# The first half's normalized input kept in DRAM across the turn of a hybrid SSD and S5 block

## The chip, the cores and the metric

One core of a Trainium2 chip runs the whole kernel. Its engines are TensorE (PE, with its weight loads shown as PEld), VectorE (DVE), ScalarE (ACT), GpSimd (POOL) and SyncE (SP, which here only issues DMAs). Each works through its own queue in order, and waits on semaphores for the others. The metric is the device time of one execution, in microseconds (us); lower is better.

## The reference

One encoder block on 2048 tokens of width 1024, all in float32:

```
h  = RMSNorm(x) * norm_w
p  = h @ W_in                    # columns: SSD z | SSD x,B,C | dt fwd,bwd | S5 u
y1 = SSD heads: conv(x,B,C), chunked scan per direction over 16 chunks of 128 tokens,
     D skip, SiLU(z) gate, RMSNorm
y2 = S5 groups: 16 channels, 64 complex states, scan per direction, GELU, GLU, RMSNorm
x  = x + concat(y1, y2) @ W_out
x  = x + ConvGLU-FFN(RMSNorm(x))
out = RMSNorm(x)
```

The change touches only how h reaches the product with W_in a second time.

## The kernel before

A product in float32 precision is made of three products of two-part numbers: each operand is split into a high part (`hh`, `wh`) and a low part (`hl`, `wl`), and lines L444 to L446 multiply high with high, low with high and high with low. The tiles `ht = (hh, hl)` hold both parts of h, transposed (128 partitions, 8 blocks of features, 1026 tokens), that is, one half of the sequence at a time. There is room for one pair only.

**Stage one.** `norm_block` (L479) takes 512 tokens: it loads four tiles of x, normalizes them, transposes them on PE (L500) and writes the high part from ACT (L503) and the low part from DVE (L504). It runs for blocks 0 and 1, then for blocks 2 and 3, which overwrite the tiles; after each block `u_dt` computes the S5 input and the SSD step sizes. At its end `ht` holds tokens 1024 to 2047, half 1.

**Half 1.** `group` (L804) runs for four groups. Each has four `conv_tile` (projection, convolution, SiLU; L672), then eight `ssd_unit` (L741), one for each chunk, from the last chunk backwards. `z_tile` (L698) projects the gate. A unit loads `rw` (two tiles of 256 KB, L747) and `eb` (L751) on SP's queue, adds a mask to `rw` (L753, on DVE in half 1), takes the exponential on ACT (L764), and then PE, DVE and ACT pass its pieces on: transposes `ptb` (L756, L757), `pyd` (L770, L776), `pst` (L791), stores `y_d` (L783) and `sf_d` (L796), again on SP's queue. `rw` and `eb` have two buffers.

**The S5 recurrence.** Beside half 1, POOL runs `recur`: 126 steps of four operations each (L347 to L350) on the array `s5V`. Then `store_states` writes `s5V` to DRAM with 16 DMAs of 256 KB that POOL issues (L356).

**The turn.** `norm_again` (L506, called for two blocks at the end of half 1) makes h of tokens 0 to 1023 again: x is loaded (L519) into tiles borrowed from others (`xa`, `zt`, `wraw`, `rb`), scaled by the kept factors (L522, L524), transposed (L529) and split (L532 on ACT, L533 on DVE). `xa` has a pool of its own, `s5xa`, which is opened within the same scope as `s5V`.

**Half 0.** The pool `s5o` is opened when the scope of `s5V` and `xa` has ended, and takes the same space. `out_setup` loads `s5gw` into it (L364, eight DMAs on SP's queue), and `outputs`, called eight times through half 0, loads `s5tz`, `s5st`, `s5uTo` and `s5ot` (L375 to L384, SP's queue) and multiplies them on PE (`s5py`, L386; `s5pgl`, L400). Groups and gate tiles run as in half 1, now on tokens 0 to 1023. Then come the output product and the FFN, which are not touched.

**What sets the order.** The code above is not the order on the engines. A scheduler places every instruction by a simulated timeline and by priorities (`tc.high_priority`), when the data and, in that timeline, the space of its tile are free; what it finds is each engine's fixed queue. On the chip an engine then waits at the head of its queue, whatever stands behind.

Of the kernel before, what the change touches and what calls it, by code (L numbers as in the profile page):

```python
# [9 lines left out]
F32 = mybir.dt.float32  # L10
F32R = mybir.dt.float32r
I32 = mybir.dt.int32
AF = mybir.ActivationFunctionType
ALU = mybir.AluOpType
# [3 lines left out]
P = 128  # L18
L = 2048
D = 1024  # L20
# [396 lines left out]
class Block:  # L417
# [40 lines left out]
    def dram(self, dr):  # L458
        t = lambda name, shape, dt=F32: dr.tile(shape, dt, name=name)
        self.ud = t("u_d", [NG5, 2, P, P])  # L460
        self.ys_d = t("ys_d", [S5W, 2, 8, P])
        self.acs_d = t("acs_d", [16, 32, P])
        self.eac_d = t("eac_d", [16, 32, P])
        self.dec_d = t("dec_d", [16, 32])
        self.ct_d = t("ct_d", [4, P, L])
        self.y_d = t("y_d", [16, P, 8, P])
        self.z_d = t("z_d", [8, P, L])
        self.sf_d = t("sf_d", [16, P, 4, 256])
        self.x2_d = t("x2_d", [L, D])
        self.hop_d = [t(f"hop{i}_d", [P, 8, 4, 512]) for i in range(2)]  # L470
        self.act_d = t("act_d", [P, self.NF, L])
        self.wt_d = t("wt_d", [P, 11, 4, 512])
        self.yp_d = [t(f"yp{i}_d", [L, D]) for i in range(2)]


    def new_ht(self, pool):
# [26 lines left out]
            nc.scalar.activation(hi, pt, AF.Copy, scale=w)  # L503
            nc.vector.scalar_tensor_tensor(lo, pt, w, hi.bitcast(F32), ALU.mult, ALU.subtract)  # L504

    def norm_again(self, xp, wp, ps, ht, tb, off):  # L506
        nc = self.nc
        xt = []
        for i in range(4):
            if i == 0:  # L510
                t = xp.tile([P, D], F32, name="xa")
            elif i == 1:
                t = wp.tile([P, D], F32, name="zt", bufs=1)
            elif tb == 0:
                t = wp.tile([P, D], F32, name="wraw", bufs=2)
            else:
                t = self.rbp.tile([P, 1028], F32, name="rb", bufs=2)[:, 0:D]
            r0 = 512 * tb + 128 * i
            nc.sync.dma_start(t, self.A["x"][0, r0:r0 + 128, :])  # L519
            r = self.rs0[:, 4 * tb + i:4 * tb + i + 1]  # L520
            if i % 2:
                nc.vector.tensor_scalar(t, t, r, None, ALU.mult)  # L522
            else:
                nc.scalar.activation(t, t, AF.Copy, scale=r)  # L524
            xt.append(t)
        for k in range(8):
            pt = ps.tile([P, 512], F32, name="pt0", tag="mm")
            for i in range(4):
                nc.tensor.transpose(pt[:, 128 * i:128 * i + 128], xt[i][:, 128 * k:128 * k + 128], self.ident)  # L529
            w = self.nmw[:, k:k + 1]  # L530
            hi, lo = ht[0][:, k, off:off + 512], ht[1][:, k, off:off + 512]
            nc.scalar.activation(hi, pt, AF.Copy, scale=w)  # L532
            nc.vector.scalar_tensor_tensor(lo, pt, w, hi.bitcast(F32), ALU.mult, ALU.subtract)  # L533

    def u_weights(self, sp, wp):
        nc = self.nc
# [671 lines left out]
def hybrid_block_kernel(ctx: ExitStack, tc: tile.TileContext, *aps):  # L1208
    nc = tc.nc
    A = dict(zip(_INS, aps[:-1]))  # L1210
    b = Block(nc, tc, A, aps[-1])
    pool = tc.tile_pool
# [5 lines left out]
    with ExitStack() as mix:  # L1218
# [6 lines left out]
        ps, p5 = (psg.enter_context(pool(name=n, bufs=2, space=PSUM)) for n in ("psmm", "ps5"))  # L1225
# [3 lines left out]
        wp = lw.enter_context(pool(name="wp", bufs=1))  # L1229
# [3 lines left out]
        ht = b.new_ht(hp)  # L1233
# [3 lines left out]
        with pool(name="s0", bufs=1) as sp, right("s5cs") as cs:  # L1237
            with right("s5prm") as sr:
                b.norm_block(sp, wp, pp, ht, 0, 2)
                b.u_weights(sp, wp)  # L1240
                p0 = tc.cur_priority
                soon = lambda: tc.high_priority(offset=tc.cur_priority - p0)
                b.u_dt(sp, ps, ht, 0, 2)
                with soon():
                    b.norm_block(sp, wp, pp, ht, 1, 514)
                b.u_dt(sp, ps, ht, 1, 514)
                with soon():
                    for i in range(2):
                        nc.scalar.copy(ht[i][:, :, 0:2], ht[i][:, :, 1024:1026].bitcast(F32))
                for j in (2, 3):  # L1250
                    with soon():
                        b.norm_block(sp, wp, pp, ht, j, 512 * j - 1022)
                    b.u_dt(sp, ps, ht, j, 512 * j - 1022)
                with soon():
                    s5.params(cs, sr)
                    b.main_consts(mk, sr, s5.pst)
            with right("s5tab") as wk:
                with soon():
                    for k in range(NK5):
                        s5.tables(wk, k)  # L1260
                for m in range(ZA):
                    b.z_tile(wp, ps, ht, 1, m)
        late = rs.enter_context(right("late"))
        mp = rs.enter_context(right("mp"))
        with pool(name="s5v", bufs=1) as vp, ExitStack() as xs:
            off = tc.cur_priority - p0
            with tc.high_priority(offset=off), pool(name="dts", bufs=1) as sp:
                b.dt_stage(late, sp, ps)
                with pool(name="s5vw", bufs=1) as wk:
                    s5.toeplitz(*[wk.tile([P, 1024], F32, name="s5xi", bufs=3)[0:16, 0:512].rearrange(  # L1270
                        "p (g o) -> p g o", o=16) for _ in range(2)])
                    s5.inputs(vp, wk)
            sp = rs.enter_context(right("sp"))
            xp = xs.enter_context(pool(name="s5xa", bufs=1))
            b.masks(late)
            b.sb = late.tile([P, 4, 256], F32, name="sb")
            p0 = tc.cur_priority
            for g in range(GA):
                if g == GA - 1:
                    p3 = tc.cur_priority  # L1280
                b.group(mp, wp, sp, ps, pp, ht, 1, g)
                for m in ZB[g]:
                    b.z_tile(wp, ps, ht, 1, m)
            p1 = tc.cur_priority
            s5.recur(vp, lambda j: tc.high_priority(offset=tc.cur_priority - p0 - int(RS * (p1 - p0) * j / P)))
            s5.store_states()
            with tc.high_priority(offset=tc.cur_priority - p3):
                for j in range(2):
                    b.norm_again(xp, wp, ps, ht, j, 2 + 512 * j)
        with right("s5o") as so:  # L1290
            s5.out_setup(so)
            for g in range(4):
# [20 lines left out]
        ps = psb.enter_context(pool(name="psb", bufs=4, space=PSUM))  # L1313
# [70 lines left out]
```

## Time and profile before

| | us |
|---|---|
| median of 3 runs (2914.89 to 2917.51) | 2915.84 |
| the profiled execution | 2897.39 |
| its span in the trace | 2895.6 |
| PE busy in it | 2691.0 (93%) |
| DVE busy | 2192.7 (76%) |
| ACT busy | 1362.3 (47%) |
| POOL busy | 656.6 (23%) |

The trace is of the profiled execution, whose span is 1.8 us shorter than its time. Busy shares are means over stages with different limits; what counts for this change is the stretch of some 150 us around the turn, read engine by engine. In the views a row of a timeline is: start, duration, engine, line, operation, output tile and input tiles, and how many were joined into the row; brackets at its end give how long the engine had been idle before it, and for whom it waited.

### The profile page before, as it was taken

What the parts mean: (1) busy time and instruction counts of PE and PEld (TensorE: products, weight loads), DVE (VectorE), ACT (ScalarE), POOL (GpSimd) and SP (SyncE); (2) the same over time, 40 slices, a digit from 0 to 9 for tenths busy, and PEclk for the clock granted to TensorE, in tenths of its full rate; (3) what the DMA queues carried; (4) which work ended last, traced back from release to release, by engine and by line L of the source; (5) the groups of instructions that cost most, each with busy time, mean ns of one, the idle gap of its engine ahead of it and who ended that gap; (6) DMA issues with size and microseconds to landing.
All of it is one profiled execution on the core that took longest, in us unless ns stands there. A gap on an engine that the chain in (4) does not pass through costs nothing. (4 is left out here: it accounts for less than half of the span.)

```text
span 2895.6 us, 37272 instructions
## 1 busy us (share of the span) xinstructions
PE 2691.0 (93%) x12952; PEld 2177.5 (75%) x12952; DVE 2192.7 (76%) x3247; ACT 1362.3 (47%) x2325; POOL 656.6 (23%) x1133
## 2 busy tenths in 40 slices
PE   6998899876999998899899999999999999999998
PEld 4666899765877886677777878787877777778786
DVE  5997589887786786667786777778877788675775
ACT  4542454445566665433335444445444445242443
POOL 0443499993233232111111000000000000000011
PEclk9999999988999999999999999999999999999999
DMA  4546534348466666967865234326433336564643
GB/s 131 175 132 199 171 106 126 110 137 225 132 179 171 176 181 180 243 190 191 247 193 180 80 109 138 102 80 196 144 132 127 122 130 225 191 234 167 219 145 124
DMA packets 504168, 466.30 MB, mean 161 GB/s; under 512 B 90204, under 2 KB 415148, under 8 KB 503980
## 3 DMA queue, kind: packets, MB, share of 16 engines
q1 hardware_dynamic: 501740, 458.75, 52.2%
q0 software_dynamic: 2240, 5.18, 0.7%
q8 instruction: 102, 1.67, 0.2%
q14 instruction: 86, 0.70, 0.1%
HBM read 321.22 MB, written 142.58 MB: 160 GB/s over the span
## 5 line engine op out<-in xcount | busy, mean ns | idle before, releaser
L1044 PE MATMUL pA<-th,lh 128*128 128x512 f32 x1056 | 422.8, 401 | 18.3 <-ACT pc L1092 16.7
L1044 PE MATMUL pA<-tl,lh 128*128 128x512 f32 x1056 | 421.5, 399 | 2.0 <-DVE tl L1031 2.0
L1044 PE MATMUL pA<-th,ll 128*128 128x512 f32 x1056 | 420.2, 399 | 0.0
L444 PE MATMUL pmm<-hh,wh 128*128 128x512 f32 (+1 forms) x896 | 333.7, 372 | 3.0 <-DVE zt L706 1.9
L445 PE MATMUL pmm<-hl,wh 128*128 128x512 f32 (+1 forms) x896 | 332.7, 371 | 0.0
L446 PE MATMUL pmm<-hh,wl 128*128 128x512 f32 (+1 forms) x896 | 330.4, 369 | 0.0
L1044 PEld LDWEIGHTS pA<-th,lh 128*128 128x128 f32 x1056 | 200.5, 190 | 74.2 <-ACT pc L1092 23.7
L1044 PEld LDWEIGHTS pA<-tl,lh 128*128 128x128 f32 x1056 | 200.4, 190 | 50.9 <-DVE tl L1031 3.1
L1044 PEld LDWEIGHTS pA<-th,ll 128*128 128x128 f32 x1056 | 200.4, 190 | 48.5
L1044 PE MATMUL pB<-tl,lh 128*128 128x512 f32 x528 | 209.7, 397 | 2.6 <-DVE tl L1031 2.6
L1044 PE MATMUL pB<-th,lh 128*128 128x512 f32 x528 | 209.6, 397 | 1.3 <-ACT th L1030 1.2
L1044 PE MATMUL pB<-th,ll 128*128 128x512 f32 x528 | 209.3, 396 | 0.0
L1092 ACT COPY pc<-pA 128x512 f32<-128x512 f32 x204 | 116.1, 584 | 177.1 <-PE pA L1044 175.7
L444 PEld LDWEIGHTS pmm<-hh,wh 128*128 128x128 f32 x896 | 169.8, 190 | 29.0 <-DVE zt L706 3.1
L445 PEld LDWEIGHTS pmm<-hl,wh 128*128 128x128 f32 x896 | 169.7, 189 | 22.4 <-issue 2.5
L446 PEld LDWEIGHTS pmm<-hh,wl 128*128 128x128 f32 x896 | 169.7, 189 | 21.1 <-issue 1.1
L764 ACT ACTIVATE Lt<-rw,tokS 128x128 f32<-128x128 f32 x512 | 157.4, 389 | 57.7 <-PE pyd L770 46.9
L692 DVE SCALAR_TENSOR_TENSOR xbc<-rb,cw,xbc 128x1024 f32<-128x1024 f32 x128 | 179.8, 1407 | 4.0 <-ACT xbc L690 3.0
L444 PE MATMUL p<-wo,yh 128*128 128x512 f32 x384 | 157.6, 410 | 22.0 <-ACT yh L439 21.0
L440 DVE TENSOR_TENSOR ll<-s,lh 128x1024 fp32r<-128x1024 f32 (+3 forms) x134 | 124.6, 931 | 51.7 <-PE pA L1044 44.2
L439 ACT CAST lh<-s 128x1024 fp32r<-128x1024 f32 (+3 forms) x134 | 107.2, 814 | 116.3 <-DVE s L1011 54.6
L445 PE MATMUL p<-wo,yh 128*128 128x512 f32 x384 | 155.7, 405 | 0.0
(421 smaller groups left out, 6126.1 us busy)
## 6 DMA issues: line engine op xcount, KB each, us to landing
wr<-in_ffn_w_up_dram SPq DMA_DIRECT2D x86, 512.0 KB
rw<-acs_d SPq DMA_DIRECT2D x128, 256.0 KB
wraw<-in_w_in_dram SPq DMA_DIRECT2D x52, 512.0 KB
ar<-act_d SPq DMA_DIRECT2D x32, 512.0 KB
tst<-hop_d SPq DMA_DIRECT2D x28, 512.0 KB
yp_d<-cv SPq DMA_DIRECT2D x28, 512.0 KB
cv<-yp_d SPq DMA_DIRECT2D x28, 512.0 KB
act_d<-cv SPq DMA_DIRECT2D x22, 512.5 KB
```

The costliest lines, as they stand in the source:

```text
L439: self.nc.scalar.copy(hi, src)
L440: self.nc.vector.tensor_tensor(lo, src, hi.bitcast(F32), ALU.subtract)
L444: mm(ps, lhs[0], rhs[0], start=first, stop=False)
L445: mm(ps, lhs[0], rhs[1], start=False, stop=False)
L446: mm(ps, lhs[1], rhs[0], start=False, stop=last)
L692: nc.vector.scalar_tensor_tensor(ac, rb[:, j:j + 1024], cw(j), ac, ALU.mult, ALU.add)
L764: nc.scalar.activation(Lt[:, d, h], rw[:, d, h], AF.Exp, bias=tk(0, d, h))
L1044: mm(ps, x, y, start=first and k == i == 0, stop=k == kt - 1 and i == 2, skip_group_check=not first)
L1092: self.nc.scalar.copy(t, src)
```

## The change

Eight DRAM tensors `h_d` of 1 MB each are added. After `norm_block` 0 and after `norm_block` 1, `h_store` writes both parts of the block to them, in four DMAs that ACT issues. At the turn `h_load` reads them back into `ht`, four DMAs for each block, that SP issues. `norm_again` and the pool `s5xa` are gone: with them 4 MB of loads of x, 8 scalings, 64 transposes on PE, 16 splits on ACT and 16 on DVE. Every later line number falls by 18.

```diff
+        self.h_d = [[[t(f"h{i}{j}{q}_d", [P, 4, 512]) for q in range(2)] for j in range(2)] for i in range(2)]
...
-    def norm_again(self, xp, wp, ps, ht, tb, off):
...
-            nc.sync.dma_start(t, self.A["x"][0, r0:r0 + 128, :])
...
-                nc.tensor.transpose(pt[:, 128 * i:128 * i + 128], xt[i][:, 128 * k:128 * k + 128], self.ident)
...
-            nc.scalar.activation(hi, pt, AF.Copy, scale=w)
-            nc.vector.scalar_tensor_tensor(lo, pt, w, hi.bitcast(F32), ALU.mult, ALU.subtract)
+    def h_store(self, ht, tb, off):
+        for q in range(2):
+            for i in range(2):
+                self.nc.scalar.dma_start(self.h_d[tb][i][q], ht[i][:, 4 * q:4 * q + 4, off:off + 512].bitcast(F32))
+
+    def h_load(self, ht, tb, off):
+        for q in range(2):
+            for i in range(2):
+                self.nc.sync.dma_start(ht[i][:, 4 * q:4 * q + 4, off:off + 512].bitcast(F32), self.h_d[tb][i][q])
...
+                b.h_store(ht, 0, 2)
                 b.u_dt(sp, ps, ht, 0, 2)
                 with soon():
                     b.norm_block(sp, wp, pp, ht, 1, 514)
+                    b.h_store(ht, 1, 514)
...
-            xp = xs.enter_context(pool(name="s5xa", bufs=1))
...
                 for j in range(2):
-                    b.norm_again(xp, wp, ps, ht, j, 2 + 512 * j)
+                    b.h_load(ht, j, 2 + 512 * j)
```

The order of the instructions changes with it. On SP's queue, in the third group of half 1, before:

```order
L751 DMA eb<-eac_d 64x2x128 x2
L796 DMA sf_d<-sf 128x256
L783 DMA y_d<-yy 128x256 x2
L747 DMA rw<-acs_d 128x512 x2
L519 DMA wraw<-in_x_dram 128x1024
L747 DMA rw<-acs_d 128x512 x2
```

The same place on SP's queue after the change:

```order
L733 DMA eb<-eac_d 64x2x128 x2
L778 DMA sf_d<-sf 128x256
L765 DMA y_d<-yy 128x256
L364 DMA s5gw<-in_s_glu_w_dram 16x32x32 x8
L375 DMA s5tz<-s5td 128x1x384 x4
L378 DMA s5st<-s5vd 128x8x128
L765 DMA y_d<-yy 128x256
L380 DMA s5uTo<-u_d 128x8x128
L384 DMA s5ot<-s5od 128x2x256 x2
L729 DMA rw<-acs_d 128x512 x2
L642 DMA wraw<-in_w_in_dram 128x8x128
```

The loads for the S5 outputs (L364 to L384) now stand between the two stores of `y_d`, ahead of the `rw` loads of the next unit. Before, they stood on SP's queue at the end of the turn:

```order
L751 DMA eb<-eac_d 64x2x128 x2
L364 DMA s5gw<-in_s_glu_w_dram 16x32x32 x8
L783 DMA y_d<-yy 128x256
L796 DMA sf_d<-sf 128x256
L751 DMA eb<-eac_d 64x2x128 x2
L747 DMA rw<-acs_d 128x512 x2
L783 DMA y_d<-yy 128x256
L375 DMA s5tz<-s5td 128x1x384 x4
L378 DMA s5st<-s5vd 128x8x128
L380 DMA s5uTo<-u_d 128x8x128
L384 DMA s5ot<-s5od 128x2x256 x2
L747 DMA rw<-acs_d 128x512
```

The new loads of h stand on SP's queue behind four more units' loads and stores (`L729` is now the `rw` load, `L515` the load of h):

```order
L729 DMA rw<-acs_d 128x512 x4
L515 DMA hl<-h_d 128x4x512
L515 DMA hh<-h_d 128x4x512
L642 DMA wraw<-in_w_in_dram 128x8x128
L778 DMA sf_d<-sf 128x256
L733 DMA eb<-eac_d 64x2x128 x2
L515 DMA hh<-h_d 128x4x512
L765 DMA y_d<-yy 128x256
L515 DMA hl<-h_d 128x4x512 x2
L515 DMA hh<-h_d 128x4x512
L515 DMA hl<-h_d 128x4x512
L515 DMA hh<-h_d 128x4x512
```

The first of the eight `s5gw` loads carries the waits for the new use of the space of `s5V`: for the last step of the recurrence (L350) and for all 16 stores of the states (L356), in both kernels; before, it also waited for the last transpose that reads `xa` (L529). On PE's queue 29 of the 64 units of `ssd_unit` (counted at `pyd<-Lt`) stand ahead of the first projection of half 0 before, and 22 after; behind the last projection stand 4 units before and 8 after.

## Rows read from the trace of the kernel before

**Rows 1.** By stretch: busy PE, PEld, DVE, ACT, POOL; PE clock; DMA share; GB/s.
```profile
40.00:50.00 10.00, 7.62 (x37) 5.94 (x37) 9.90 (x64) 5.24 (x8) 0.00 (x0) 0.96 0.79 271
50.00:60.00 10.00, 10.00 (x40) 8.05 (x39) 6.43 (x31) 5.49 (x9) 2.00 (x6) 0.87 0.16 47
...
640.00:700.00 60.00, 29.89 (x167) 23.05 (x168) 43.75 (x78) 28.92 (x68) 28.59 (x50) 0.72 0.77 207
700.00:760.00 60.00, 60.00 (x283) 48.30 (x282) 48.28 (x70) 27.09 (x51) 13.69 (x12) 1.00 0.60 152
...
900.00:1000.00 100.00, 97.42 (x543) 81.21 (x542) 77.86 (x120) 63.83 (x123) 33.88 (x32) 1.00 0.66 180
...
1120.00:1182.00 62.00, 38.08 (x222) 31.67 (x220) 38.72 (x70) 34.87 (x60) 9.66 (x14) 0.87 0.77 235
```

**Rows 2.** PE's timeline: half 1's last projection matmul, half 0's first.
```profile
621.16 0.40 PE L446 MATMUL pmm<-hh,wl 128*128 128x512 f32 x1
...
699.76 0.48 PE L444 MATMUL pmm<-hh,wh 128*128 128x512 f32 x1
```

**Rows 3.** Operations of norm_again, by line.
```profile
L529 PE MATMUL pt<-ident,xa x16: 271/421/479, 620.8 to 696.4; 128*128 128x128 f32 x16
...
L533 DVE SCALAR_TENSOR_TENSOR hl<-pt,nmw,hh x16: 735/745/754, 641.7 to 700.2; 128x512 fp32r<-128x512 f32 x16
```

**Rows 4.** SP's DMA queue where the changed order begins.
```profile
553.21 21.40 SPq L783 DMA_DIRECT2D y_d<-yy  x2
576.13 0.80 SPq L747 DMA_DIRECT2D rw<-acs_d  x2
```

**Rows 5.** The recurrence's last operation: all, one stretch, and two neighbouring steps.
```profile
L350 POOL TENSOR_TENSOR s5V<-s5V,s5r x126: 356/427/1431, 328.6 to 658.9; 128x64 f32<-128x64 f32 x126
...
584.00:660.00 76.00, 18.15 (x32) 0.82 0.45 134
...
605.08 0.35 POOL L347 TENSOR_TENSOR s5r<-s5V,s5ar 128x64 f32<-128x64 f32 x1
...
606.64 0.35 POOL L347 TENSOR_TENSOR s5r<-s5V,s5ar 128x64 f32<-128x64 f32 x1
```

**Rows 6.** The stores of the states, by line, with the time to landing.
```profile
L356 POOL DMA_DIRECT2D s5vd<-s5V x16: 687/687/875, 659.6 to 674.7; - x16
...
DMA to landing us min/median/max: 6.7/9.1/11.7
```

**Rows 7.** SP's DMA queue: rw loads, and the loads for the S5 outputs.
```profile
604.69 5.48 SPq L747 DMA_DIRECT2D rw<-acs_d  x4
...
696.78 4.05 SPq L364 DMA_DIRECT2D s5gw<-in_s_glu_w_dram  x8
...
706.17 2.62 SPq L375 DMA_DIRECT2D s5tz<-s5td  x4
...
716.00 0.41 SPq L747 DMA_DIRECT2D rw<-acs_d  x1
```

**Rows 8.** DVE's mask adds, and PE at the unit they feed (timelines).
```profile
585.35 0.68 DVE L753 TENSOR_TENSOR rw<-rw,msk 128x512 f32<-128x512 f32 x1
...
609.31 0.69 DVE L753 TENSOR_TENSOR rw<-rw,msk 128x512 f32<-128x512 f32 x1 [4.94 <-DMA rw<-acs_d]
...
590.88 0.61 PE L776 MATMUL pyd<-xbc,sb 128*128 128x128 f32 x4
```

**Rows 9.** A unit's matmuls on PE, timeline.
```profile
657.51 0.55 PE L756 MATMUL ptb<-ident,xbc 128*128 128x128 f32 x3
...
658.12 0.60 PE L791 MATMUL pst<-xw,xb 128*128 128x256 f32 x2
...
660.43 0.66 PE L770 MATMUL pyd<-Lt,xb 128*64 128x128 f32 x8 [1.17 <-DVE yy L781]
...
662.00 0.27 PE L529 MATMUL pt<-ident,xa 128*128 128x128 f32 x1
```

**Rows 10.** ACT in stage one, waiting for x of the second block (timeline).
```profile
47.27 1.06 ACT L489 ACTIVATE zt<-xt 128x1024 f32<-128x1024 f32 x1 [3.25 <-DMA xt<-in_x_dram]
```

More of the change, by code (lines that the diff above doesn't have):

```diff
@@ L504, in norm_block @@
             nc.vector.scalar_tensor_tensor(lo, pt, w, hi.bitcast(F32), ALU.mult, ALU.subtract)
-    def norm_again(self, xp, wp, ps, ht, tb, off):
[L507 to L518, printed above, removed]
-            nc.sync.dma_start(t, self.A["x"][0, r0:r0 + 128, :])
[L520 to L528, printed above, removed]
-                nc.tensor.transpose(pt[:, 128 * i:128 * i + 128], xt[i][:, 128 * k:128 * k + 128], self.ident)
-            w = self.nmw[:, k:k + 1]
-            hi, lo = ht[0][:, k, off:off + 512], ht[1][:, k, off:off + 512]
-            nc.scalar.activation(hi, pt, AF.Copy, scale=w)
-            nc.vector.scalar_tensor_tensor(lo, pt, w, hi.bitcast(F32), ALU.mult, ALU.subtract)
+    def h_store(self, ht, tb, off):
[6 more added lines that the diff above has]
+                self.nc.sync.dma_start(ht[i][:, 4 * q:4 * q + 4, off:off + 512].bitcast(F32), self.h_d[tb][i][q])
     def u_weights(self, sp, wp):
```

## The prediction

> **What bounds the kernel now.** I read the busy shares by stretch first [rows 1]. In half 0 PE is the bound: busy 60.00 of 60 us in 700 to 760 and 97.42 of 100 in 900 to 1000. At the turn it is not: 29.89 of 60 us in 640 to 700, at a mean granted clock of 0.72, between the two levels of 1.2 and 2.4 GHz. PE's timeline shows the same gap from its ends [rows 2]: the last projection matmul of half 1 starts at 621.16, the first of half 0 at 699.76, 79 us later. In between PE does units and the transposes of `norm_again`, one small piece at a time. The recomputation in itself is little: 64 transposes of some 0.42 us or less are under 27 us of PE, and 16 splits of 0.745 are 12 us of DVE [rows 3]. So what the change can win directly is a part of that gap. What it may cost is read from SP's and POOL's rows, because the diff and the order show that far more is moved than removed.
>
> **Part 1: the loads for the S5 outputs move up, and SP stops there.** With the pool of `xa` gone the scheduler believes the space of `s5V` free earlier, and puts `s5gw` to `s5ot` ahead of two thirds of what SP still has to issue for half 1. The first `s5gw` load waits for POOL's last L350 and for the 16 state stores. In the run of before SP is at that place at 553.21 [rows 4]; POOL finishes L350 at 658.9 [rows 5] and the last store is issued at 674.7 and takes 9.1 us to land [rows 6]. So SP must stand still for about 100 us, and behind it stand the `rw` loads that before were issued at 576.13 [rows 4], and every later `rw`, `eb`, `y_d` and weight.
>
> Who waits for that: DVE's queue reaches the mask add of that `rw` at 585.35, and PE the unit it feeds at 590.88 [rows 8]. Both stop, since their queues are in order and each `rw` has only two buffers. ACT follows.
>
> When does SP go on? POOL has 32 of its 126 steps left at 584 [rows 5]. Beside a busy DVE they took 76 us, 2.37 each. While DVE waited (its add at 609.31 came after 4.94 us of idling [rows 8]), one step took 606.64 - 605.08 = 1.56 us [rows 5]. In the stall DVE is idle all the time, so I take 1.56: 32 x 1.56 = 50, and POOL ends at 634; the other end is 660, as now. The Trainium skill ("SBUF — State Buffer", SBUF: two separate sides) says that DVE and GpSimd share one port pair as an exclusive lock; the two step times here agree with that, and by it the end would be 634, without it 660.
>
> After POOL: the stores take 674.7 - 659.6 + 0.7 = 15.8 to issue and 9.1 to land (6.7 to 11.7) [rows 6]: 659. SP then issues `s5gw` in 4.05 and the other S5 loads in 716.00 - 706.17 = 9.8 [rows 7]: 673. `rw` needs some 4.6 us from its issue at 604.69 to the add at 609.31 [rows 7, 8]: 678. So DVE goes on at 678 in the state that it had at 585. PE then has what it had between 590.88 and 621.40, 30.5 us, and starts some 2.5 us after DVE: half 1's projections end at 711, and half 0's first matmul, whose h chases the last readers, starts there, 11 us later than the 699.76 of now. **Term: +11.** All short ends (634, landing 6.7, the S5 loads in half the time) give 664 for 678 and -2; all long ends (660, 11.7) give 706 and +40.
>
> **Part 2: units that are still owed.** In the new order 22 units stand ahead of half 0's first matmul on PE, 29 before. Seven units have to be done later. On PE a unit is 662.00 - 660.43 = 1.57 plus 658.12 - 657.51 = 0.61 [rows 9], 2.18 us. Since PE is the bound in half 0 [rows 1], this is not hidden: 7 x 2.18 = **+15**.
>
> **Part 3: the loads of h.** They are 8.4 MB. The highest rate in these rows is 271 GB/s, at the turn it was 207 [rows 1]: 31 to 41 us. The pieces are released one by one by the last gate tile of half 1, from about 702 on, so they are in by 733 to 743. PE meanwhile has the owed 15 us and the projections for pieces that have come. It lacks between 0 and 20 us of work, depending on how the order interleaves them; I take **+6**, near the lower end, since in 700 to 760 PE had no idle time at all beside a DMA share of 0.60 [rows 1]. The removed transposes, splits and x loads earn nothing beyond this: they lay in the gap that is already counted as 79 us of before and about 120 of after.
>
> **Part 4: the end of half 0.** Before, four units stand behind the last projection, and in 1120 to 1182 PE is idle 62 - 38.08 = 24 us [rows 1], waiting for units and S5 outputs that have no projection to hide them. In the new order eight units stand there. If the idle time grows with the units it is +24, if S5 outputs cover the four extra ones it is 0: **+12**, the middle, for lack of a nearer row.
>
> **Part 5: the stores in stage one.** Four stores of 1 MB go out ahead of the second block's x loads, for which ACT already waits 3.25 us until 47.27 [rows 10]; the DMA engines are 0.79 busy at 271 GB/s then, and 0.16 in the ten us after [rows 1]. If the stores go first, 4.2 MB at 271 GB/s is 15 us, of which some 12 would show on ACT; if the x loads keep their share, 0: **+6**. The other four fall in the empty stretch. The Trainium skill ("DMA: Bandwidth & Descriptors", Issuing engines are not separate DMA queues) says that DMAs from all issuing engines run on the same 16 engines and interleave, and that another queue saves only issue time. That speaks against the stores being free on ACT's queue: by it this term lies between 6 and 12, by the opposite view at 0; no row here shows two queues at once in this stretch.
>
> **Sum:** 11 + 15 + 6 + 12 + 6 = +50 us on the profiled execution of 2897.39, so 2947. The runs' median, 2915.84, is 18 us higher than the profiled execution; the same step on it gives **2966**.
>
> **The rivals.**
>
> *A, the forecast:* SP stops at the first S5 load. +50. All short ends together give -2 + 15 + 0 + 0 + 0 = +13, all long ends 40 + 15 + 20 + 24 + 12 = +111; the long ends hardly come together, and I stop at +94.
>
> *B, the stall is longer than derived.* POOL does not speed up while DVE waits, because its steps are slow by themselves, and the loads of h find no cover. For it speaks that the median L350 is 0.43 and not 0.35 [rows 5]; against it the steps beside an idle DVE. 40 + 15 + 20 + 12 + 12 = +99.
>
> *C, half 0 absorbs what the stall costs.* The owed units fit into the 24 us in which PE idles before 1182 and the tail does not grow: +11 + 6 = +17, and with the short stall +4. For it: DVE has 22 us in 100 to spare in half 0 [rows 1]. Against it: PE has 2.6.
>
> *D, the other side: SP does not have to wait.* The deciding point is where POOL stands when SP comes to `s5gw`. If POOL were done and its states stored by 553 to 585, SP would pass, half 1 would end at 621 as now and half 0 start about 10 us later, once its first h pieces have landed: 631 for 700, a gain of 69, less 15 for the owed units, 20 for loads that nothing covers, 12 at the end and 6 in stage one: -16, and -35 if the last two terms vanish. POOL's 32 missing steps at 584 speak against it: it would have to be 100 us ahead of now, and nothing is taken from POOL before that.
>
> *E, the change does little:* the scheduler's new order costs as much at one end as it gives at the other, the recomputation being hidden work: within 6 us. The row of SP at 553.21 speaks against it.
>
> **How the numbers follow.** Chances: A 0.70, B 0.08, C 0.10, D 0.08, E 0.04. The prediction is A's, 2966. For 8 in 10 the range takes A's bounds, +13 to +94, the cut C shares with A, and a little below for the two: 2924 (+8) to 3010 (+94). Outside stay D, E, a third of C and most of B. A measurement of this kernel can tell about 0.2%, 6 us. Faster by more: D and a little of E, 0.09. Within 6 us: most of E and a third of C, 0.06. Slower by more: the rest, 0.85.
>
> **What would show it.** In the new trace SP's queue should have an L364 row that is preceded by about 100 us without any issue, beginning near 553 and ending near 660. DVE and PE should idle from about 586 and 591 until 675, PE waiting last for DVE or for the `rw` load, at the low clock when it restarts. L350 should end near 634, with steps of 1.6 us in that stretch. Half 0's first 512-wide L444 should start near 711, and eight units should follow the last projection, with more than 24 us of idle PE. The prediction is wrong if SP gets past L364 before 600, if POOL is far ahead of its present pace at 553, or if PE finds enough other work in its queue while `rw` is missing. It is too low if the loads of h come one behind the other with long gaps, since they stand on the same queue as the `rw` loads of the owed units; each of those that waits for a buffer holds back an h piece.

## The result and the profile after

The changed kernel takes 2986.64 us (median of 4 runs, 2981.37 to 2992.80), the kernel before 2915.36 beside it (2912.14 to 2917.51): a ratio of 1.0242, 95% interval 1.0225 to 1.0259, so 71 us slower. The forecast was 2966 with a range of 2924 to 3010.

The profiled execution of the changed kernel is 2985.49 us, its span 2983.7, that is 88 us more than the span of before. The two figures differ because the profiled execution of before, 2897.39, was 18 us under its median, while that of after was not; beside the experiments the kernel before ran between 2895.19 and 2915.20. Sizes of single steps below are from the traces and sum to 88; kernels are compared by the medians of their runs.

SP's queue, changed kernel (start, duration, line, DMA):

```profile
566.08 0.38 SPq L765 DMA_DIRECT2D y_d<-yy  x1
667.55 4.04 SPq L364 DMA_DIRECT2D s5gw<-in_s_glu_w_dram  x8
671.63 2.61 SPq L375 DMA_DIRECT2D s5tz<-s5td  x4
```

Nothing is issued for 101 us. In the rows of before SP issued at 553.21 and 576.13 in this place [rows 4], and came to `s5gw` at 696.78 [rows 7]. DVE and PE of the changed kernel, from their timelines (idle time and releaser in brackets):

```profile
580.16 0.29 DVE L662 MEMSET rb<- 128x2 f32 x2
667.59 0.29 DVE L366 TENSOR_REDUCE s5bm<-ident 128x8 f32<-128x128 f32 x1 [87.15 <-DMA s5vd<-s5V]
...
687.02 0.69 DVE L735 TENSOR_TENSOR rw<-rw,msk 128x512 f32<-128x512 f32 x1 [7.09 <-DMA rw<-acs_d]
```

```profile
585.43 0.32 PE L446 MATMUL pmm<-hh,wl 128*128 128x342 f32 x1
668.53 0.70 PE L752 MATMUL pyd<-Lt,xb 128*64 128x128 f32 x4 [82.78 <-DVE Lt L749]
```

```profile
729.11 0.39 PE L446 MATMUL pmm<-hh,wl 128*128 128x512 f32 x1
729.34 0.61 PE L386 MATMUL s5py<-s5st,s5ot 128*128 128x127 f32 x4
730.98 0.50 PE L444 MATMUL pmm<-hh,wh 128*128 128x512 f32 x1 [1.03 <-DMA hh<-h_d]
```

PE stands for 83 us at the end of a chain that begins with POOL's state stores (`s5vd`): DVE waits for them at a small reduction, `s5bm`, and PE for DVE. The wait for `rw` that SP's stop brings comes after it, 7.09 us until 687.02. The row at 729.11 is half 1's last projection matmul, 730.98 half 0's first; before they were at 621.16 and 699.76 [rows 2]. POOL, by line, and two neighbouring steps in the stop:

```profile
L350 POOL TENSOR_TENSOR s5V<-s5V,s5r x126: 354/371/1455, 343.3 to 643.7; 128x64 f32<-128x64 f32 x126
```

```profile
611.38 0.34 POOL L347 TENSOR_TENSOR s5r<-s5V,s5ar 128x64 f32<-128x64 f32 x1
...
612.94 0.34 POOL L347 TENSOR_TENSOR s5r<-s5V,s5ar 128x64 f32<-128x64 f32 x1
```

The recurrence starts 15 us later than before (343.3 for 328.6) and still ends 15 us earlier (643.7 for 658.9) [rows 5], because its steps take 1.56 us while DVE stands (612.94 - 611.38). By stretch, columns as in rows 1, the stop, half 0 up to its last projection, and the end of half 0:

```profile
553.00:668.00 115.00, 21.81 (x123) 20.11 (x121) 23.68 (x37) 12.26 (x26) 90.35 (x217) 0.61 0.26 60
730.00:1175.00 445.00, 423.90 (x2255) 345.28 (x2256) 323.06 (x538) 249.54 (x519) 117.45 (x102) 0.98 0.61 167
1175.00:1272.00 97.00, 54.72 (x309) 41.64 (x307) 66.45 (x115) 53.98 (x106) 23.64 (x22) 0.80 0.72 200
```

The kernel before in the stretches that answer to the last two:

```profile
700.00:1120.00 420.00, 412.73 (x2224) 339.30 (x2223) 316.16 (x501) 254.72 (x502) 121.27 (x114) 1.00 0.60 165
```

Its end is the row 1120 to 1182 in [rows 1]. So the span's 88 us lie like this, by the edges of these stretches: half 0 begins 30 us later (730 for 700), its projections take 25 us longer (445 for 420), its end 35 us longer (97 for 62), and what follows is 2 us shorter.

### The profile page after: what moved, and what is told of

Its sections match the earlier page's. It is cut to its first block, busy times and chain, and to the rows that moved or that the text cites. A ratio compares the mean times of both kernels' runs of the same rounds, so it can differ in the third digit from the quotient of the medians.

```text
span 2983.7 us, 37105 instructions
## 1 busy us (share of the span) xinstructions
PE 2681.5 (90%) x12888; PEld 2162.9 (72%) x12888; DVE 2164.8 (73%) x3227; ACT 1338.3 (45%) x2298; POOL 638.3 (21%) x1133
## 5 line engine op out<-in xcount | busy, mean ns | idle before, releaser
L444 PE MATMUL pmm<-hh,wh 128*128 128x512 f32 (+1 forms) x896 | 336.8, 376 | 11.2 <-DVE zt L688 7.4
L444 PEld LDWEIGHTS pmm<-hh,wh 128*128 128x128 f32 x896 | 171.5, 191 | 39.1 <-DVE zt L688 8.3
L444 PE MATMUL p<-wo,yh 128*128 128x512 f32 x384 | 157.7, 411 | 23.3 <-ACT yh L439 22.8
L674 DVE SCALAR_TENSOR_TENSOR xbc<-rb,cw,xbc 128x1024 f32<-128x1024 f32 x128 | 172.4, 1356 | 5.5 <-ACT xbc L672 4.6
```

What stands on the lines that cost most here:

```text
L444: mm(ps, lhs[0], rhs[0], start=first, stop=False)
L674: nc.vector.scalar_tensor_tensor(ac, rb[:, j:j + 1024], cw(j), ac, ALU.mult, ALU.add)
```

## The experiments

The change and ten kernels, with the ratio to the kernel before that ran beside them:

| run | median us | before | ratio, 95% interval |
|---|---|---|---|
| the change | 2986.64 | 2915.36 | 1.0242 (1.0225 to 1.0259) |
| e1_stores | 2918.05 | 2906.66 | 1.0046 (1.0027 to 1.0065) |
| e2_gate | 2919.59 | 2906.66 | 1.0049 (1.0028 to 1.0071) |
| e3_xa_apart | 2978.55 | 2906.66 | 1.0248 (1.0225 to 1.0271) |
| e4_stores_sp | 2909.99 | 2904.93 | 1.0021 (1.0005 to 1.0036) |
| e5_gate_late | 2927.96 | 2906.66 | 1.0072 (1.0049 to 1.0096) |
| e6_bm | 2994.78 | 2904.93 | 1.0319 (1.0297 to 1.0340) |
| e7_pool_loads | 2961.33 | 2904.93 | 1.0205 (1.0184 to 1.0225) |
| e8_gate_mid | 2888.85 | 2904.93 | 0.9948 (0.9929 to 0.9967) |
| e9_before_bm | 2912.56 | 2904.06 | 1.0026 (1.0013 to 1.0039) |
| e10_mid_no_bm | 2895.06 | 2904.06 | 0.9961 (0.9939 to 0.9983) |

### Is it h in DRAM, or the loads that moved?

The kernel before, with only the place of one pool changed:

```diff
-            xp = xs.enter_context(pool(name="s5xa", bufs=1))
+            xp = rs.enter_context(right("s5xa"))
```

> The kernel before, with h made again as it was and no stores, but with the pool of xa on the other side of the memory, so that the S5 output tiles no longer wait for it. The S5 loads move up on SP's queue as in the changed kernel (20 units ahead instead of 32). Theory: the moved loads alone are the loss: SP stops at about 550 until some 655 to 665, and the time grows by 50 to 75 us, to 2965 to 2990. Rival: the loss belongs to the stores and loads of h; then it stays within 6 us of 2915.

1.0248, the loss of the whole change, without a byte of h stored or loaded and with `norm_again` in full. Its SP queue:

```profile
556.83 0.38 SPq L783 DMA_DIRECT2D y_d<-yy  x1
653.01 4.03 SPq L364 DMA_DIRECT2D s5gw<-in_s_glu_w_dram  x8
```

96 us without an issue. The pool of `xa` had been holding the S5 loads back, and without it in their way the stop comes with h made again as before. The rival that the loss belongs to the stores and loads of h has fallen; what the stores alone cost is asked further down.

The opposite edit, the changed kernel with that pool back and POOL writing one column of it from the last loaded piece of h:

```diff
+            xp = xs.enter_context(pool(name="s5xa", bufs=1))
...
+                xa = xp.tile([P, D], F32, name="xa")
+                nc.gpsimd.tensor_copy(xa[:, 0:1], ht[1][:, 7, 1025:1026].bitcast(F32))
```

> The changed kernel with the pool of xa back: one column of it is written by POOL from the last piece of h that is loaded, and nothing else is done with it. So the S5 loads can stand on SP's queue only behind the loads of h (27 units' rw loads ahead of them, 20 in the changed kernel, 32 before). Theory: the stop moves from about 566 to behind the h loads and shrinks to what is then left of POOL's recurrence, some 0 to 40 us, while PE has half 0's projections: 30 to 80 us faster than the changed kernel, 2905 to 2955. Rival: the loads of h on SP's queue or the stores are what costs; then it stays within 15 us of the changed kernel's 2987.

1.0049: of 71 us some 57 are gone. A shorter stop is left, since the last piece of h is issued at 638.15 and POOL's last L350 comes only at 669.2; DVE's timeline of this run:

```profile
693.31 0.29 DVE L366 TENSOR_REDUCE s5bm<-ident 128x8 f32<-128x128 f32 x1 [43.20 <-DMA s5vd<-s5V]
```

### Which of the queues holds the others?

The row of `s5bm` in the changed kernel was not foreseen: a reduction of 0.29 us in the same space, in DVE's queue, with the same wait. It was moved into another pool, where it is done early:

```diff
-        self.bm = wk.tile([P, 8], F32, name="s5bm")
+            s5.bm = late.tile([P, 8], F32, name="s5bm")
```

> The changed kernel with the small reduction s5bm (which stands in DVE's queue in the same space as the S5 loads and also waits for the state stores) moved into another pool, so that DVE is held by nothing but data. SP still comes to the S5 loads after 20 units. Theory: SP's stop is the cause by itself, DVE then waits for rw instead; only the order of stage one is better by the way (73 projection steps ahead of the last S5 input product instead of 86), 5 to 13 us: 2970 to 2985. Rival: DVE's wait at s5bm is the cause; then the gap of PE shrinks by half or more and the time falls below 2950.

1.0319, not faster than the change but 22 us slower against the common reference. DVE's and PE's timelines:

```profile
679.95 0.69 DVE L732 TENSOR_TENSOR rw<-rw,msk 128x512 f32<-128x512 f32 x1 [93.30 <-DMA rw<-acs_d]
```

```profile
677.77 1.19 PE L383 MATMUL s5py<-s5uTo,s5tz 128*128 128x256 f32 x2 [89.42 <-DMA s5uTo<-u_d]
```

Without `s5bm` DVE waits for `rw`, as the prediction had it, and PE stands at a third lock: its own queue has the first S5 output matmul (`s5py`) ahead of the rest of half 1. So DVE's wait was one of three that lead to the same event, and removing it brings nothing. Why it became slower is not settled; its order differs at several places (18 units ahead of `s5py`, 19 in the change).

Next SP was freed as well, the S5 loads of the setup and of the first block being issued by POOL behind its own stores:

```diff
-            nc.sync.dma_start(self.gw[16 * t:16 * t + 16].rearrange("p g v o -> p g (v o)"), gsrc)
+            nc.gpsimd.dma_start(self.gw[16 * t:16 * t + 16].rearrange("p g v o -> p g (v o)"), gsrc)
...
+        ld = nc.sync if b else nc.gpsimd
```

> As the run without s5bm in the way, and the S5 loads of the setup and of the first output block are issued by POOL, behind its own state stores, so that SP does not stop either. What is left in the queues ahead of its time is PE's first S5 output matmul, now behind 22 units and 512 projection steps (19 and 488 in the changed kernel, 32 and 568 before). Theory: the stop moves to PE and becomes shorter, from when half 1's projections are done until about 690: 2900 to 2930, 50 to 80 us faster than the changed kernel. Rival: SP's stop was not the cause; then 2960 or more.

1.0205: the stop did move to PE, but it is long, and my estimate of 2900 to 2930 was 30 us too low; 2961 lies where the rival had put it (2960 or more). PE's timeline:

```profile
631.52 0.39 PE L444 MATMUL pmm<-hh,wl 128*128 128x512 f32 x1
701.34 1.19 PE L384 MATMUL s5py<-s5uTo,s5tz 128*128 128x256 f32 x2 [69.44 <-DMA s5ot<-s5od]
```

Half 1's last convolution is out of PE at 620.6, its last projection at 631.5; then PE stands 69 us at `s5py`. SP issues up to 643.40 and DVE works up to 638.7 in this run; then DVE stands for PE (68.3 us) and SP for ACT (59.4 us), whose data come from PE. So the cost does not hang on SP's stop alone: with SP and DVE free the same event holds them through PE. I had placed that stop within the gap of 79 us that the kernel before has anyway, but before, units ran in that gap, and here they wait behind it. So an instruction that is hoisted takes its consumers along, and every queue in which one of them stands is held.

### Is the stop all there is?

The gate was moved further back, to the state after half 0's first group (`e5_gate_late`), and to that group's last convolution tile (`e8_gate_mid`, which also has `s5bm` apart and the stores issued by SP). For this the first group is written ahead of the S5 setup in both, so the order changes there too. The core of the latter:

```diff
+            sl = b.group(mp, wp, sp, ps, pp, ht, 0, 0)
+            xa = xp.tile([P, D], F32, name="xa")
+            nc.gpsimd.tensor_copy(xa[:, 0:1], sl[3][:, 0:1])
```

> As the run with the gate, but the gate reads the SSD state that the last unit of half 0's first group leaves, so the S5 loads stand behind all of that group (43 units' rw loads ahead of them). Theory: SP never waits for the recurrence; half 0 starts near 640 to 660 instead of 700, 7 owed units cost 15 us, the loads of h some 20 uncovered, the tail 6 units for 4 some 18, stage one 6 to 15: between 20 us faster and 20 us slower than the kernel before, 2895 to 2935, and 20 us or more faster than the earlier gate if that one still stops. Rival: without the stop the h loads turn out to be the next wait and the time stays above 2950.

> The changed kernel with the stores on SP, s5bm in another pool, and a gate on the pool of xa that reads the last convolution tile of half 0's first group, so that the S5 loads (36 units ahead) and the first S5 output matmul (33 units and 637 projection steps ahead) come to their place at about 690 or later. Stage one has 70 projection steps ahead of the last S5 input product, fewer than before. Theory: no queue stops for the recurrence, half 0 starts at 625 to 640, five units instead of four are left at the end: equal to the kernel before or up to 30 us faster, 2880 to 2912. Rival: half 0 gains nothing from an earlier start, because its units and outputs need POOL, which is busy with the recurrence and the stores until 675 to 690; then within 10 us above the kernel before.

The late gate gives 1.0072, no better than the early one, which I had expected it to beat by 20 us: no queue stops, but the S5 outputs come late (first `s5py` at 893.7, before at 745.5), and in 760 to 800 PE is busy for only 24.57 of 40 us, its longest wait, 12.49 us, being for DVE's convolution (`xbc`). That S5 outputs would have filled it is argued, not shown. The middle one gives 0.9948 (0.9929 to 0.9967), 16 us faster than the kernel before, and by the two ratios some 85 faster than the change. By stretch:

```profile
640.00:700.00 60.00, 50.29 (x241) 39.71 (x240) 43.77 (x71) 26.53 (x57) 26.53 (x43) 0.94 0.78 197
700.00:760.00 60.00, 46.33 (x234) 36.23 (x233) 45.12 (x71) 26.68 (x62) 13.94 (x8) 0.93 0.41 127
```

PE is busy 50 us in 640 to 700, where it was 30 [rows 1], so the gap at the turn is really closed; half 0's first copy out of a projection is at 633.8 instead of 706.1. But these 72 us are given back: 700 to 760 falls from 60.00 to 46.33, PE's longest wait, 10.18 us until 760.92, again being for DVE's convolution, and seven units are owed as in the change. The output product starts at 1181.1, before at 1181.9. So by place half 0 gained nothing from its earlier start, as the rival had it, though the time came out as the theory had it. The spans of these two traces differ by 9 us, nearly all of it behind that point, where no run has an edit; what lies behind it takes 1705 us here, 1714 before, and between 1705 and 1724 in the twelve traces. The source of the 16 us is therefore not shown, and no run has the gate with h made again, which would tell what belongs to h in DRAM. Two controls for `s5bm`:

```diff
-        self.bm = wk.tile([P, 8], F32, name="s5bm")
+            s5.bm = late.tile([P, 8], F32, name="s5bm")
```

> The kernel before with s5bm alone moved into another pool; h is still made again. Its order keeps 76 projection steps ahead of the last S5 input product, 32 units ahead of the S5 loads and 4 behind the last projection. It tells how much of the 16 us that the mid gate run gains over the kernel before belongs to h in DRAM at all. Theory: nothing here was late because of s5bm, since before it stands behind the recurrence anyway: within 6 us of the kernel before. Rival: the gain of the mid gate run comes from s5bm: 8 us or more faster.

> The mid gate run with s5bm back in its place in the pool of the S5 outputs; stage one then has 76 projection steps ahead of the last S5 input product, as the kernel before, where the mid gate run has 70. Theory: the gate alone keeps all queues free, s5bm stands behind the recurrence too, and what is lost is the better order of stage one, six steps of 0.7 us: 2890 to 2900, 5 to 15 us faster than the kernel before. Rival: s5bm still holds DVE at the turn, visible as a wait of DVE on the state stores of more than 10 us; then equal to the kernel before or slower.

The kernel before with `s5bm` apart is a little slower (1.0026, 8 us, more than the 6 I had allowed), and the middle gate with `s5bm` in its old place is still faster (0.9961). So `s5bm` is not the source of the gain.

### What do the stores cost?

The kernel before with the eight stores and nothing else, first issued by ACT as in the change, then by SP (the last pair of lines is what differs between the two runs):

```diff
+                b.h_store(ht, 0, 2)
...
-                self.nc.scalar.dma_start(self.h_d[tb][i][q], ht[i][:, 4 * q:4 * q + 4, off:off + 512].bitcast(F32))
+                self.nc.sync.dma_start(self.h_d[tb][i][q], ht[i][:, 4 * q:4 * q + 4, off:off + 512].bitcast(F32))
```

> The kernel before with the eight stores of h in stage one alone; h is still made again at the turn, and nothing reads the stores. Theory: the stores cost stage one its share of the loss, some 6 us (0 to 12 was the bound) or up to the 15 us by which the recurrence starts later in the changed kernel (343.3 for 328.6), and S5 loads still stand at the end of the turn: 2921 to 2931 us, and SP without a stop of 100 us. Rival: the later start of the recurrence is no effect of the stores but of the trace of before, whose profiled execution lay 18 us under the median; then the time is that of the kernel before within 6 us.

> The kernel before with the same eight stores, issued by SP instead of ACT. The traffic is that of the run with the stores alone, which lost 13 us; the order is not: with the stores on ACT 86 projection steps of three matmuls stand on PE ahead of the last S5 input product, on SP 76, as in the kernel before. Theory: the loss is the order, ten gate projections of 0.7 us that delay the S5 inputs and with them the recurrence; here it is gone, the recurrence starts at 329 to 332 and the time is within 6 us of the kernel before. Rival: the loss is the traffic, 8.4 MB in the first 100 us; then it stays at 8 to 15 us and the recurrence starts after 338.

1.0046 from ACT, 13 us, and 1.0021 from SP, 6 us. The recurrence's last line, first in e1, then in e4:

```profile
L350 POOL TENSOR_TENSOR s5V<-s5V,s5r x126: 354/427/1442, 342.0 to 673.8; 128x64 f32<-128x64 f32 x126
```

```profile
L350 POOL TENSOR_TENSOR s5V<-s5V,s5r x126: 357/428/1447, 329.4 to 660.3; 128x64 f32<-128x64 f32 x126
```

The traffic is the same, so it is not what delays the recurrence; the late start of 342 is gone with the order in which 76 projection steps, not 86, stand ahead of the last S5 input product. That it is the order, and not ACT's issuing, is borne out by `e6_bm`: its stores are issued by ACT, 73 steps stand ahead, and its recurrence starts at 333.3. Ten steps of some 0.7 us are 7 of the 12.6 us; the rest is not placed. Nor is what the late start costs: e1 and e4 reach the output product together (1196.3 and 1197.4, before 1181.9), and the intervals of their ratios overlap. What the 6 us of e4 are, traffic or order further on, stays open: its trace is 3 us behind before at half 0's start (709.3 for 706.1) and 15 us at the output product.

The Trainium skill ("DMA: Bandwidth & Descriptors", Issuing engines are not separate DMA queues) says that issuing DMAs from another engine saves only the time of issuing them. No run here tests that by itself: between e1 and e4 the order on PE changed with the queue.

## Why the prediction was right, and where not

**The mechanism** was right in its origin, and the direction with it: the S5 loads moved up, and SP's stop at the first `s5gw`, foreseen from 553 to 660, came from 566 to 668. That the move is the cause is shown by e3 (the stop without h in DRAM) and e2 (h in DRAM with a shorter stop). The way from there to PE was only in part as foreseen. SP's queue is one of three that wait for the same event; the other two were missed: `s5bm` in DVE's queue, and `s5py` in PE's. In the changed kernel DVE and PE stood for `s5bm`; the wait for `rw` that the prediction named holds DVE for the whole stop only in e6, where the time did not fall. What each of the three costs by itself no run shows, but e7 shows that freeing SP and DVE is not enough.

**POOL's speed in the stop** was right: 1.56 us a step, as read from the one place where DVE waited [rows 5]. The Trainium skill ("SBUF — State Buffer", SBUF: two separate sides) calls the port pair that DVE and GpSimd share an exclusive lock; steps of 1.56 us beside a standing DVE and 2.37 beside a busy one [rows 5] agree with it. So rival B's condition did not come. But L350 ended at 643.7 and not at 634: the recurrence had started 15 us later, and 41 steps were left when DVE stopped, not 32.

**Term by term**, from the traces: the start of half 0 was to be 11 us later and stage one 6, together 17; it is 30. PE went on at 668.53, 12 us earlier than the 680 of the prediction, since DVE was let go by the landing of the stores and not by `rw`; but it then needed 61 us for what was left of half 1, and not 30.5. So the state in which the stop was entered was mis-sized. The prediction took PE at 590.88 as it was before; but PE had done less by then. Projection steps by L444 up to the stop, changed kernel (the time, then PE's busy time and count), and before:

```profile
0.00:585.80 585.80, 206.19 (x575) 110.02 (x575) 0.96 0.53 155
```

```profile
0.00:590.80 590.80, 214.62 (x601) 114.39 (x601) 0.96 0.49 144
```

26 steps of some 0.7 us are 18 us, and three units fewer were done (16 for 19), some 7 us at the 2.18 of the prediction. How much of that is stage one is not shown: its bound of 12 us asked only what the traffic could do to ACT's waits and did not look at what the stores do to the order; e1 and e4 show the order's part in the later start of the recurrence.

The owed units and the loads of h were to be 15 + 6 = 21; the stretch is 25 us longer. The sum is near, but by luck. Of the seven owed units only three are done in this stretch (34 for 31), the other four at the end; PE is busy 11 us longer (423.90 for 412.73) and idle 14 us longer (21 for 7). That idle time is not the loads of h, which are hidden, PE's wait for h being the 1.03 us at 730.98; 9.9 us of it stand before two S5 output matmuls (`s5py`), with no releaser that the profile shows.

The end was to be +12 and is +35. PE idles 97.00 - 54.72 = 42 us there, 24 before: the idle time grew by 18, half-way between the middle that was taken and the upper end of 24. The other 17 us are work, 54.72 us for 38.08, at a mean clock of 0.80 for 0.87; the term had none of it, since the prediction had counted the owed units' work earlier. This is the term that was sized worst.

Sum: 17 + 21 + 12 = 50 foreseen, 30 + 25 + 35 - 2 = 88 in the traces, 71 in the medians. The time lies in the range, but 88 for 50 in the traces is further off than the medians show. Two slips in the prediction's arithmetic change nothing in this: all short ends of part 1 give 668 and not 664, so some +1 and not -2, and D without its last two terms is -34, not -35.

**The rivals.** C, that half 0 absorbs it, fell: the end grew. E, that the order does little, fell with e3. D, that the queues do not stop, did not happen in the change. e8 is that case made on purpose, and D's price of -16 is what e8 measures; but e8 also has other edits, and its trace shows no gain at the output product, where D's terms would all be in. The agreement is luck as far as the runs show.

## What to carry to other kernels

When an edit removes a buffer, look at what had been waiting for that buffer's space: with a scheduler that works from a simulated timeline, a wait that seemed to be waste can be what holds later loads behind the work that must come first. Compare the order of each queue, and for every instruction that has moved up ask what it waits for on the chip, which queue it stands in, and where its consumers now stand; the waits go with them. Recomputing something in a stretch where the bound engine idles anyway should be cheap, and taking it away should gain at most the part of the gap that the work owed from before does not fill; this last point is argued here, since no run takes the recomputation away and leaves the order as it was.

## What was not expected of the hardware

That PE restarts at its lower clock after such a stop was foreseen; how a stop of queues looks in the busy shares was not. The run `e6_bm` shows both most plainly, by stretch, columns as in rows 1:

```profile
600.00:640.00 40.00, 0.00 (x0) 0.00 (x0) 0.00 (x0) 0.00 (x0) 33.92 (x98) 0.50 0.05 11
...
700.00:720.00 20.00, 20.00 (x114) 16.72 (x113) 13.89 (x26) 10.60 (x28) 0.00 (x0) 1.00 0.62 207
```

While PE does nothing the granted clock is 0.50, the level of 1.2 GHz; in 700 to 720, with PE busy throughout, it is 1.00, that of 2.4 GHz. In `e7_pool_loads` the first matmuls after the stop still show the lower level: an L443 takes 0.63 us at 702.76 and 0.39 before the stop. The same rows of `e6_bm` show POOL alone at work in the stop, 33.92 of 40 us, and the DMA engines all but idle (0.05), though PE, DVE, ACT and SP all had work left in their queues: a stop of queues looks in the busy shares like a lack of work.
